# Seven block products in place of eight for every other pair of row tiles in an MLP's second product

## The chip, the cores and the metric

One core of a Trainium2 chip runs the whole program. The metric is the device time of one execution in microseconds (us). The kernel before took 634.06 us (median of 3 runs, 633.57 to 634.90). One more execution was recorded by the profiler; every row below is from it.

## The reference

Two layers of a decoder trunk on one sequence of 256 tokens with 1024 channels, in float32. Each layer adds an attention mixer's output and then an MLP's output to x. The change is in the MLP:

```python
def sqrelu_mlp(hn, w1, w2):
    return jnp.square(jax.nn.relu(hn @ w1)) @ w2
...
x = x + mix
x = x + sqrelu_mlp(rms_norm(x, norm_mlp[i]), mlp_w1[i], mlp_w2[i])
```

`w1` is 1024 x 4096 and `w2` is 4096 x 1024. Layer 0's mixer joins sparse and differential attention, layer 1's is block-sparse attention; both have an input and an output projection.

## The kernel before, in words

**Numbers in two parts.** Every operand of a matmul is split into a high part, which the matmul's format holds exactly, and a low rest. A product a·b is then three matmuls into one PSUM bank: ah·bh, ah·bl and al·bh (`mm3`, L532 to L536). For a weight block of 128x1024 the split is one ScalarE copy to `whi` (L475) and one VectorE subtraction to `wlo` (L478), in `splits`. Pairs of such tiles are slots (`parts`, six of them, and spare halves of `mT` or `xT`, which is why some rows say `mTh`/`mTl` for a weight). `loads` (L452) brings the blocks, 512 KB each, through SP's queue into five `raw` tiles in the order in which `_blocks` lays them out.

**The MLP** (`mlp`, L1357). The 4096 hidden channels are 16 tiles of 256. The first product makes a tile's hidden values transposed, 256 channels by 256 tokens, in one bank: two columns of 128 channels, each 8 steps of `mm3` with 256 columns moving, 48 matmuls (`cols_T`, L614). `square` (L1362) then takes the bank through ReLU (ScalarE), the square's high part (ScalarE, L1370), the whole square (GpSimd, L1371) and the low part (VectorE, L1373). The second product takes a tile's 256 rows of `w2` as two blocks of 128x1024. With two halves of 128 tokens (t) and two halves of 512 output columns (n) that is 2 x 2 x 2 = 8 block products of 128x128 by 128x512, each one `mm3`: 24 matmuls into four banks, one for each (t, n) (`row_mm`, L684). The rows of tile i follow the first product of tile i + 1. The last three tiles (`TAIL`) are kept back and are done (t, n) by (t, n), so that each bank is added to x (`add_to_x`, L1303) and the next stage can begin on it.

**What sets the order.** The program is written once as generators, and a planner (`Plan`) plays it through when the kernel is built: each step has an engine, a cost, what it depends on and an urgency; of the ready steps an engine takes the lowest urgency first. What comes out is a fixed order for each engine. Weight splits have urgency -1 when they are needed soon (`URGENT`) and 3 otherwise. In `out_proj` (L1316), which ends a mixer, the rows of tokens 128 to 255 have the urgency 1 + `LATER[layer]` against 1 for the others (L167, L1341).

**The start.** Until weights are there, TensorE multiplies zeros (`WARM`, L502, and `keep_on`, L907, one at a time at the lowest urgency and an assumed 0.23 us each).

Of the kernel before, what the change touches and what calls it, by code (L numbers as in the profile page):

```python
# [21 lines left out]
F32 = mybir.dt.float32  # L22
# [51 lines left out]
def _blocks(ins):  # L74
# [44 lines left out]

    def mlp(l):  # L120
        up, down = f["mlp_w1"][l], f["mlp_w2"][l]
        last = FF // 256 - TAIL
        out.extend([n(up, 0, 4, span(0, 512)), n(up, 4, 8, span(0, 512)), r(down, 0)])
# [4 lines left out]
        out.extend(r(down, i) for i in range(last, FF // 256))  # L128

# [8 lines left out]
    cut = []  # L138
    for b in out:
# [3 lines left out]
    return cut  # L143


def _lay_out(ins):
    f = {k: np.asarray(ins[k]) for k in ins}
    blocks = _blocks(ins)
# [9 lines left out]
    for i, nm in enumerate(("ev_lam_q1", "ev_lam_q2", "ev_lam_k1", "ev_lam_k2")):  # L158
# [3 lines left out]
            "prm": prm, "gs": gs, "cst": _constants(), "eye": np.eye(128, dtype=np.float32)}, [b.shape[1] for b in blocks]  # L162
# [4 lines left out]
SECOND, ROOM, LATER = 5, (4, 5), (0, 0.05)  # L167
# [148 lines left out]
class Slots:  # L316
# [5 lines left out]
    def get(self, n=1):  # L322
        ev = Event()
        self.waiting.append((ev, n))
# [25 lines left out]
    def serve(self):  # L350
        while self.waiting and len(self.items) >= self.waiting[0][1]:
            ev, n = self.waiting.pop(0)
            got, self.items = self.items[:n], self.items[n:]
# [10 lines left out]
def trunk_kernel(ctx: ExitStack, tc: tile.TileContext, x, w, prm_d, gs, cst_d, eye, out, widths):  # L364
    nc = tc.nc

# [62 lines left out]
    class Piece:  # L429
        count, current, uses = 0, 0, 0  # L430

        def __init__(self):
            self.p, self.ready, self.slots = Piece.count, Event(), parts
            Piece.count += 1

        def use(self):
            Piece.current = max(Piece.current, self.p)
            Piece.uses += 1

# [20 lines left out]

    def splits():
        for p, n in enumerate(widths):
            pc = pieces[p]
            yield loaded[p]
            got = pc.slots.get()
# [416 lines left out]
    KL = acts.tile([128, 2, 2, S], F32R, name="KL")  # L882
    KZ = acts.tile([128, 2, 2, S], F32R, name="KZ")
# [17 lines left out]
    def first_norms():  # L901
        def keep_on():
# [3 lines left out]
            while Piece.uses < KEEP:  # L906
                yield pe(0.23, lambda: nc.tensor.matmul(banks[1].t, z[:, :128], z, start=True, stop=True), u=9)  # L907
# [449 lines left out]
    def mlp(src, x_ready, nxt):  # L1357

        NI = FF // 256
        hs = [Event() for _ in range(NI)]  # L1360

        def square(i, b, deps, slots):  # L1362
            got = pbuf.get(2)
            tgot = tbuf.get()
            yield [got, tgot]
            r, sq = got.value
            hh, hl = tgot.value
# [223 lines left out]
```

## Time and profile before

| | us |
|---|---|
| median of 3 runs | 634.06 |
| the profiled execution | 634.41 |
| its span in the trace | 632.6 |
| TensorE busy | 620.1 |
| VectorE busy | 404.5 |
| ScalarE busy | 361.7 |
| GpSimd busy | 80.4 |

The profiled execution's own time is 1.8 us over its span, which is the time around the first and last instruction. A row of the timeline gives an instruction's start and duration; the duration reaches past the moment at which the engine takes the next instruction, so starts that follow each other are closer than durations say. Line numbers are those of the listing above.

### The profile page before, as it was taken

How to read it: one execution, taken by the hardware profiler on the slowest of the kernel's cores; microseconds unless marked ns; L12 is line 12 of the kernel's file. 1: busy time of each engine (PE TensorE's matmuls, PEld its weight loads, DVE VectorE, ACT ScalarE, POOL GpSimd, SP SyncE). 2: the span in 40 equal slices, each digit the busy share in tenths (PEclk: the TensorE clock that was granted, in tenths of full speed). 3: DMA queues.
4: the chain of work that ended last, by engine and by line, in shares of the span. 5: the costliest groups of instructions: out<-in, count | busy, mean ns of one | idle time of the engine just before them, and what ended most of it. 6: DMA issues, size and time to landing. Idle time of an engine off the chain costs nothing.

```text
span 632.6 us, 10575 instructions
## 1 busy us (share of the span) xinstructions
PE 620.1 (98%) x4046; PEld 562.6 (89%) x4046; DVE 404.5 (64%) x722; ACT 361.7 (57%) x649; POOL 80.4 (13%) x109
## 2 busy tenths in 40 slices
PE   9999999999999999999999999999999999999995
PEld 7999989887899898998988999988889899898994
DVE  5898899868554544545467588885964454554434
ACT  5779587656644545444444488773864544445421
POOL 2031031210200101011120012010020101001111
PEclk9999999999999999999999999999999999999998
DMA  8864633426665576565626443350786556565501
GB/s 324 283 244 133 202 101 110 176 92 204 222 204 196 168 204 192 191 186 205 189 82 212 168 137 131 130 189 17 229 271 214 185 189 188 181 209 167 166 1 67
DMA packets 32274, 110.03 MB, mean 174 GB/s; under 512 B 3408, under 2 KB 5728, under 8 KB 32224
## 3 DMA queue, kind: packets, MB, share of 16 engines
q1 hardware_dynamic: 31360, 106.74, 51.7%
q0 software_dynamic: 576, 2.10, 1.0%
q8 instruction: 31, 0.51, 0.3%
q10 hardware_dynamic: 288, 0.52, 0.2%
q14 instruction: 19, 0.16, 0.1%
HBM read 108.28 MB, written 1.07 MB: 173 GB/s over the span
## 4 chain that ended last, share of the span: by engine, by line
PE 86%; DVE 7%; ACT 4%; issue 2%; POOL 1%; POOLq 0%; DVEq 0%; ACTq 0%
PE ps L535 27%; PE ps L536 27%; PE ps L534 26%; DVE wlo L478 2%; PE ps L763 2%; PE ps L797 1%; ACT P L777 1%; PE ps L597 1%; PE ps L907 1%; PE ps L502 1%; ACT whi L475 1%; DVE P L773 1%; DVE G L974 0%; DVE Tl L525 0%; DVE x L1308 0%
## 5 line engine op out<-in xcount | busy, mean ns | idle before, releaser
L478 DVE TENSOR_TENSOR wlo<-raw,whi 128x1024 fp32r<-128x1024 f32 (+1 forms) x157 | 190.3, 1220 | 71.8 <-ACT whi L475 71.3
L475 ACT ACTIVATE whi<-raw 128x1024 fp32r<-128x1024 f32 (+1 forms) x157 | 163.3, 1051 | 93.2 <-PE ps L536 62.3
L534 PE MATMUL ps<-xTh,whi 128*128 128x256 f32 x592 | 169.1, 286 | 0.0
L536 PE MATMUL ps<-xTh,wlo 128*128 128x256 f32 x592 | 166.3, 281 | 0.0
L535 PE MATMUL ps<-xTl,whi 128*128 128x256 f32 x592 | 166.2, 281 | 0.0
L535 PEld LDWEIGHTS ps<-xTl,whi 128*128 128x128 f32 x592 | 111.7, 189 | 0.6
L534 PEld LDWEIGHTS ps<-xTh,whi 128*128 128x128 f32 x592 | 111.6, 188 | 0.6
L536 PEld LDWEIGHTS ps<-xTh,wlo 128*128 128x128 f32 x592 | 111.5, 188 | 0.0
L1371 POOL TENSOR_TENSOR P<-P 128x512 f32<-128x512 f32 x32 | 35.8, 1119 | 321.5 <-ACT P L1368 321.5
L478 DVE TENSOR_TENSOR mTl<-raw,mTh 128x1024 fp32r<-128x1024 f32 x34 | 42.5, 1249 | 22.9 <-ACT mTh L475 22.9
L475 ACT ACTIVATE mTh<-raw 128x1024 fp32r<-128x1024 f32 x34 | 36.1, 1062 | 29.7 <-PE ps L535 20.3
L1368 ACT ACTIVATE P<-ps 128x512 f32<-128x512 f32 x32 | 19.1, 598 | 52.3 <-PE ps L536 52.3
L1373 DVE TENSOR_TENSOR Tl<-P,Th 128x512 fp32r<-128x512 f32 x22 | 15.2, 692 | 50.2 <-POOL P L1371 50.2
L536 PE MATMUL ps<-whi,Tl 128*128 128x512 f32 x120 | 46.9, 390 | 0.0
L535 PE MATMUL ps<-wlo,Th 128*128 128x512 f32 x120 | 46.9, 390 | 0.0
L534 PE MATMUL ps<-whi,Th 128*128 128x512 f32 x120 | 46.8, 390 | 0.0
L777 ACT ACTIVATE P<-P,nm 128x128 f32<-128x128 f32 x80 | 35.4, 446 | 14.1 <-DVE nm L773 13.9
L535 PE MATMUL ps<-xTl,mTh 128*128 128x256 f32 (+1 forms) x128 | 37.9, 296 | 1.1 <-DVE xTl L478 1.1
L534 PE MATMUL ps<-xTh,mTh 128*128 128x256 f32 (+1 forms) x128 | 38.1, 297 | 0.0
L536 PE MATMUL ps<-xTh,mTl 128*128 128x256 f32 (+1 forms) x128 | 37.8, 295 | 0.0
L534 PE MATMUL ps<-whi,xTh 128*128 128x512 f32 (+1 forms) x88 | 34.3, 390 | 0.0
L535 PE MATMUL ps<-wlo,xTh 128*128 128x512 f32 (+1 forms) x88 | 33.1, 376 | 0.0
(221 smaller groups left out, 1196.7 us busy)
## 6 DMA issues: line engine op xcount, KB each, us to landing
raw<-in_w_dram SPq DMA_DIRECT2D x192, 512.0 KB, 4.1
gB<-in_gs_dram POOLq DMA_DIRECT2D x4, 512.0 KB, 4.0
x<-in_x_dram SPq DMA_DIRECT2D x2, 512.0 KB, 5.2
B<-ud SPq DMA_DIRECT2D x1, 1024.0 KB, 7.6
B<-ud SPq DMA_DIRECT2D x2, 512.0 KB, 9.1
raw<-in_w_dram SPq DMA_DIRECT2D x2, 420.0 KB, 7.0
gB<-in_gs_dram SPq DMA_DIRECT2D x1, 512.0 KB, 5.3
out_dram<-P SPq DMA_DIRECT2D x2, 256.0 KB, 2.1
```

Source lines behind the costliest of these rows:

```text
L475: nc.scalar.activation(pc.hi[:, :n], raw[:, :n], AF.Copy)
L478: nc.vector.tensor_tensor(pc.lo[:, :n], raw[:, :n], pc.hi[:, :n].bitcast(F32), OP.subtract)
L502: pe(0.43, lambda: nc.tensor.matmul(banks[7].t, tbuf.items[1][0][:, :128], tbuf.items[1][0], start=True, stop=True), zero_e)
L534: nc.tensor.matmul(out_, ah, bh, start=start, stop=False)
L535: nc.tensor.matmul(out_, ah, bl, start=False, stop=False)
L536: nc.tensor.matmul(out_, al, bh, start=False, stop=stop)
L597: nc.tensor.transpose(p[:, 128 * k:128 * k + 128], xs[:, 128 * k:128 * k + 128], ident)
L763: nc.tensor.matmul(ps[:, 128 * qt:128 * qt + nk], q[:, par, ts], k[i][:, par, :nk], start=i == 0, stop=i == 1)
L777: nc.scalar.activation(P[:, c], P[:, c], AF.Exp, bias=nm[:, qt:qt + 1], scale=-1.0, accum_out=sums[:, qt:qt + 1])
L1368: e = act(t_act(512), lambda: nc.scalar.activation(r, b.t, AF.Relu), got, *deps)
L1371: g = pool(1.225, lambda: nc.gpsimd.tensor_tensor(sq, r, r, OP.mult), e)
L1373: h = dve(t_dve(512), lambda: nc.vector.tensor_tensor(hl, sq, hh.bitcast(F32), OP.subtract), f, g)
```

## The change

For the tiles with odd number below 13 (1, 3, 5, 7, 9, 11 of each MLP; "fused" in the code) the 2 x 2 x 2 block product is done with seven block products in place of eight. With a(t,k) the hidden blocks and b(k,n) the weight blocks, VectorE forms t1 = b01 - b00, t3 = b11 - b01, t2 = b11 - t1 and t4 = b10 - t2 in place in the raw tiles, and s1 = a10 + a11, s2 = s1 - a00, s3 = a00 - a10 and s4 = a01 - s2. The products a00·b00, a01·b10, s1·t1, s3·t3, s2·t2, s4·b11 and a11·t4 go to seven banks; an output block is the sum of some of them.

For the even tiles below 13 ("apart") the eight products remain. They go to four of the seven banks (those of b10, t4, t1 and b11); since t1's bank is added to both halves of the tokens, the product for b11's bank takes a(0,k) - a(1,k), which VectorE forms.

The rest that changes with it:

- `square` has no GpSimd step: VectorE multiplies r by r. It writes into two slots in `G0` and `G1` (`hbuf`), and splits the sums too.
- The seven banks leave one for the first product, which runs one tile further ahead; the weight blocks are laid out in that order. One more weight slot lies in `KL` and `G1` (`spare_w`).
- When a fused or apart product is over, b00's, t1's, t2's and t3's banks are added to x by 4, 2, 3 and 2 operations of 128x512 on VectorE, ahead of the last three tiles; those go into b10's, b11's and t4's banks and one fresh bank.
- A zero product at the start is planned at 0.43 us before 6.3 us.
- `LATER` for layer 1 is -0.05 in place of 0.05.

```diff
-            if i <= last:
-                out.append(r(down, i - 1))
+            if i - 2 < last:
+                out.append(r(down, i - 2))
+                if _fused(i - 2):
+                    fused.add(len(out) - 1)
...
+def _fused(i):
+    return i % 2 == 1 and i < FF // 256 - TAIL
...
-SECOND, ROOM, LATER = 5, (4, 5), (0, 0.05)
+SECOND, ROOM, LATER = 5, (4, 5), (0, -0.05)
...
+    def split_pair(p):
...
+        def place(k, names, src, deps):
+            hi, lo = k
+            n = 512 * len(names)
+            e = act(t_act(n, False), lambda: nc.scalar.activation(hi[:, :n], src, AF.Copy), *deps, u=u)
+            f = dve(t_dve(n), lambda: nc.vector.tensor_tensor(lo[:, :n], src, hi[:, :n].bitcast(F32), OP.subtract), e, u=u)
...
+        def total(dst, a, b, *deps):
+            return dve(t_dve(512), lambda: nc.vector.tensor_tensor(dst, a, b, OP.subtract), *deps, u=u)
...
+        f1 = place(k.value, ["b00"], r1[:, :512], [k, loaded[p]])
+        e1 = total(r1[:, :512], r1[:, 512:], r1[:, :512], f1)
...
+        f2 = place(k.value, ["b10", "b11"], r2, [k, loaded[p + 1]])
+        e3 = total(r1[:, 512:], r2[:, 512:], r1[:, 512:], e1, loaded[p + 1])
+        e2 = total(r2[:, 512:], r2[:, 512:], r1[:, :512], e3, f2)
+        e4 = total(r2[:, :512], r2[:, :512], r2[:, 512:], e2)
...
+        raws.put(r1, [place(k.value, ["t1", "t3"], r1, [k, e1, e3]), e2])
...
+        raws.put(r2, [place(k.value, ["t4", "t2"], r2, [k, e4])])
...
-                yield pe(0.23, lambda: nc.tensor.matmul(banks[1].t, z[:, :128], z, start=True, stop=True), u=9)
+                yield pe(0.43 if plan.now < 6.3 else 0.23, lambda: nc.tensor.matmul(banks[1].t, z[:, :128], z, start=True, stop=True), u=9)
...
-            f = act(t_act(512, False), lambda: nc.scalar.activation(hh, r, AF.Square), e, tgot)
-            g = pool(1.225, lambda: nc.gpsimd.tensor_tensor(sq, r, r, OP.mult), e)
...
-            h = dve(t_dve(512), lambda: nc.vector.tensor_tensor(hl, sq, hh.bitcast(F32), OP.subtract), f, g)
...
+            f = act(t_act(512, False), lambda: nc.scalar.activation(hh[:, :512], r, AF.Square), e, hgot)
+            e = dve(t_dve(512), lambda: v(sq, r, r, OP.mult), e, got)
+            pbuf.put(r, [f, e])
+            h = dve(t_dve(512), lambda: v(hl[:, :512], sq, hh[:, :512].bitcast(F32), OP.subtract), f, e)
...
+            if _fused(i):
+                n = 512
+                a00, a10, a01, a11 = (sq[:, 128 * j:128 * j + 128] for j in range(4))
+                s1, s2, s3, s4 = (ss[:, 128 * j:128 * j + 128] for j in range(4))
+                for dst, x_, y_, op in ((s1, a10, a11, OP.add), (s2, s1, a00, OP.subtract), (s3, a00, a10, OP.subtract),
+                                        (s4, a01, s2, OP.subtract)):
+                    e = dve(t_dve(128), lambda dst=dst, x_=x_, y_=y_, op=op: v(dst, x_, y_, op), e)
+            else:
+                n = 256
+                d = sq.rearrange("p (k t c) -> p k t c", k=2, t=2)
+                e = dve(t_dve(256), lambda: v(ss[:, :256].rearrange("p (k c) -> p k c", k=2), d[:, :, 0], d[:, :, 1], OP.subtract), e)
+            f2 = act(t_act(n, False), lambda: nc.scalar.activation(hh[:, 512:512 + n], ss[:, :n], AF.Copy), e, hgot)
+            h2 = dve(t_dve(n), lambda: v(hl[:, 512:512 + n], ss[:, :n], hh[:, 512:512 + n].bitcast(F32), OP.subtract), f2)
...
+        TERMS = (("b00", 0, (0, 1, 2, 3)), ("b10", 2, (0,)), ("t1", 4, (1, 3)), ("t3", 6, (2, 3)),
+                 ("t2", 5, (1, 2, 3)), ("b11", 7, (1,)), ("t4", 3, (2,)))
...
+        def apart(i, pcs):
...
+                       for nm, col, n in (("b10", 2 * a, 0), ("t4", 2 * a + 1, 0), ("t1", 2 * a + 1, 1), ("b11", 4 + a, 1))]
...
+        def fused(i, pc):
+            ends = []
+            for nm, col, _ in TERMS:
...
+                product(nm, i, col, op, pc.block(nm), i == LAST[nm])
...
+        for i in range(NI - 2):
+            if i + 2 < NI:
                 got = bank_a.get()
                 yield got
                 evs = [got] + [cols_T(src, got.value, next_piece(), col) for col in range(2)]
-                plan.spawn(square(i + 1, got.value, evs, bank_a))
+                plan.spawn(square(i + 2, got.value, evs, bank_a))
...
+            if i < NI - TAIL:
+                two = [next_piece(), next_piece()]
+                if _fused(i):
+                    fused(i, two[0])
+                else:
+                    apart(i, two)
...
+                def add(b=b, t=t, n=n):
+                    c = slice(512 * n, 512 * n + 512)
+                    nc.vector.scalar_tensor_tensor(X[t][:, c], b.t, rs2[t][0], X[t][:, c], op0=OP.mult, op1=OP.add)
```

TensorE issues 40 matmuls fewer (36 of 128x512 in the two MLPs and four zero products at the start), VectorE 214 operations more, ScalarE 50 more, GpSimd 32 fewer; SP's order of transfers is the same. Up to the first MLP the orders of ScalarE, VectorE and GpSimd are unchanged.

**The start, on TensorE.** L502 and L907 are the zero products of the kernel before, L589 and L998 those of the change; L597 and L684 are the transposes of the normed tokens, L534 and L621 the first matmul on weights. Before:

```order
L502 MATMUL ps7_117<-Th1_87 128x512 x10
L907 MATMUL ps1_111<-Th1_87 128x512 x10
L597 MATMUL ps4_114<-ident_121,P0_99 128x128 x4
L907 MATMUL ps1_111<-Th1_87 128x512
L597 MATMUL ps5_115<-ident_121,P1_100 128x128 x4
L907 MATMUL ps1_111<-Th1_87 128x512 x8
L534 MATMUL ps0_110<-whi0_74,xTh_104 128x280
```

and with the change:

```order
L589 MATMUL ps7_117<-Th1_87 128x512 x10
L998 MATMUL ps1_111<-Th1_87 128x512 x6
L684 MATMUL ps4_114<-ident_121,P0_99 128x128 x4
L998 MATMUL ps1_111<-Th1_87 128x512
L684 MATMUL ps5_115<-ident_121,P1_100 128x128 x4
L998 MATMUL ps1_111<-Th1_87 128x512 x7
L621 MATMUL ps0_110<-whi0_74,xTh_104 128x280
```

Six zero products stand ahead of the first transposes where ten stood, and seven in place of eight ahead of the first matmul on weights.

**Inside the first MLP, on VectorE.** Before, one tile's work between two others, L478 being the low part of a weight block and L1373 that of the hidden tile:

```order
L478 TENSOR_TENSOR mTl_91<-raw3_97,mTh_90 128x1024
L478 TENSOR_TENSOR wlo1_81<-raw4_98,whi1_75 128x1024
L478 TENSOR_TENSOR mTl_91<-raw0_94,mTh_90 128x1024
L1373 TENSOR_TENSOR Tl1_89<-P1_100,Th1_87 128x512
L478 TENSOR_TENSOR wlo2_82<-raw1_95,whi2_76 128x1024
```

and with the change the larger part of one fused tile. L1479 is the square, L1494 the four sums of hidden blocks, L1481 and L1501 the low parts of the squares and of the sums, L513 the low part of a pair of weight blocks, L522 the differences of weight blocks:

```order
L1479 TENSOR_TENSOR P4_103<-P2_101 128x512
L1494 TENSOR_TENSOR P0_99<-P4_103 128x128
L1494 TENSOR_TENSOR P0_99<-P0_99,P4_103 128x128
L1481 TENSOR_TENSOR G1_93<-P4_103,G1_93 128x512
L1494 TENSOR_TENSOR P0_99<-P4_103 128x128
L1494 TENSOR_TENSOR P0_99<-P4_103,P0_99 128x128
L513 TENSOR_TENSOR wlo5_85<-raw2_96,whi5_79 128x1024
L1501 TENSOR_TENSOR G1_93<-P0_99,G1_93 128x512
L522 TENSOR_TENSOR raw1_95<-raw2_96,raw1_95 128x512
L522 TENSOR_TENSOR raw2_96<-raw2_96,raw1_95 128x512
L522 TENSOR_TENSOR raw2_96<-raw2_96 128x512
L513 TENSOR_TENSOR wlo1_81<-raw1_95,whi1_75 128x1024
```

Ahead of these stand the low part of b00 and the first difference, and behind them the low part of t4 and t2: 15 operations for one fused tile, beside the two weight splits of the first product, where three stood.

**The end of layer 1's output projection, on TensorE.** `mTh`/`mTl` are the attention's outputs, `xTh`/`xTl` the normed tokens for the MLP, L597 and L684 the transposes that make them, and ps1 and ps0 the banks of the MLP's first product. Before, the last transposes of tokens follow twelve matmuls of that product, the last of which stand here:

```order
L534 MATMUL ps1_111<-whi2_76,xTh_104 128x512
L535 MATMUL ps1_111<-wlo2_82,xTh_104 128x512
L536 MATMUL ps1_111<-whi2_76,xTl_105 128x512
L597 MATMUL ps5_115<-ident_121,P0_99 128x128 x4
L534 MATMUL ps0_110<-whi1_75,xTh_104 128x512
```

and with the change, from the output projection's last product on:

```order
L621 MATMUL ps1_111<-whi2_76,mTh_90 128x512
L622 MATMUL ps1_111<-wlo2_82,mTh_90 128x512
L623 MATMUL ps1_111<-whi2_76,mTl_91 128x512
L621 MATMUL ps0_110<-KL_130,xTh_104 128x512
L622 MATMUL ps0_110<-G1_93,xTh_104 128x512
L623 MATMUL ps0_110<-KL_130,xTl_105 128x512
L621 MATMUL ps0_110<-KL_130,xTh_104 128x512
L622 MATMUL ps0_110<-G1_93,xTh_104 128x512
L623 MATMUL ps0_110<-KL_130,xTl_105 128x512
L684 MATMUL ps7_117<-ident_121,P2_101 128x128 x4
```

Six matmuls stand between the last output product and the last transposes where twelve stood.

## Rows read from the trace of the kernel before

**Rows 1.** Page, section 1: busy us (share of the span) and instructions per engine

```profile
PE 620.1 (98%) x4046; PEld 562.6 (89%) x4046; DVE 404.5 (64%) x722; ACT 361.7 (57%) x649; POOL 80.4 (13%) x109
```

**Rows 2.** Waits of TensorE: waiter, releaser, us in total, times, longest

```profile
PE ps L597 <- DVE P L581: 1.2, 1, 1.2
```

**Rows 3.** Windows, both MLPs: PE, PEld, DVE, ACT, POOL busy; clock; DMA share; GB/s

```profile
168.00:312.00 144.00, 144.00 (x937) 131.66 (x936) 71.44 (x65) 70.29 (x79) 14.48 (x14) 1.00 0.60 192
467.00:614.00 147.00, 147.00 (x950) 134.11 (x949) 70.79 (x66) 68.91 (x78) 15.55 (x15) 1.00 0.54 172
```

**Rows 4.** Timeline of TensorE in the first MLP: start, us, engine, line, instruction

```profile
239.84 0.39 PE L534 MATMUL ps<-whi,G 128*128 128x512 f32 x1
...
243.93 0.28 PE L534 MATMUL ps<-xTh,whi 128*128 128x256 f32 x1
...
249.61 0.40 PE L534 MATMUL ps<-mTh,Th 128*128 128x512 f32 x1
```

**Rows 5.** Lines by form, whole run: instruction, count, busy us, mean ns, idle before

```profile
L478 DVE TENSOR_TENSOR wlo<-raw,whi 128x1024 fp32r<-128x1024 f32 x154 | 187.6, 1226 | 70.8 <-ACT whi L475 70.3
...
L475 ACT ACTIVATE whi<-raw 128x1024 fp32r<-128x1024 f32 x154 | 160.9, 1055 | 90.0 <-PE ps L536 62.3 <-PE ps L535 23.5 <-issue 2.1
...
L1373 DVE TENSOR_TENSOR Tl<-P,Th 128x512 fp32r<-128x512 f32 x22 | 15.2, 692 | 50.2 <-POOL P L1371 50.2
...
L1310 DVE SCALAR_TENSOR_TENSOR x<-ps,rs,x 128x512 f32<-128x512 f32 x8 | 6.0, 749 | 11.7 <-PE ps L536 11.7
...
L525 DVE TENSOR_TENSOR mTl<-ps,mTh 128x256 fp32r<-128x256 f32 x12 | 5.0, 422 | 4.8 <-ACT mTh L519 4.5
```

**Rows 6.** Timeline of VectorE, an early 128-column operation

```profile
19.45 0.23 DVE L735 TENSOR_TENSOR lp<-prm 128x128 f32<-128x128 f32 x1
```

**Rows 7.** Timeline of VectorE, start of the second MLP's first product

```profile
448.07 2.35 DVE L478 TENSOR_TENSOR wlo<-raw,whi 128x1024 fp32r<-128x1024 f32 x2
450.33 0.68 DVE L525 TENSOR_TENSOR xTl<-ps,xTh 128x512 fp32r<-128x512 f32 x1
450.93 1.21 DVE L478 TENSOR_TENSOR wlo<-raw,whi 128x1024 fp32r<-128x1024 f32 x1
```

**Rows 8.** Tile raw, first MLP: idle before its instructions (us, times) by releaser

```profile
  PE ps L536: 29.9, 26
  ACT whi L475: 29.2, 24
```

**Rows 9.** Timeline of the first 12 us, TensorE and VectorE

```profile
5.87 3.24 PE L907 MATMUL ps<-Th 128*128 128x512 f32 x10
...
6.60 1.42 DVE L923 SCALAR_TENSOR_TENSOR P<-x,rs,gB 128x512 f32<-128x512 f32 x2 [1.71 <-DMA gB<-in_gs_dram]
...
8.95 0.60 PE L597 MATMUL ps<-ident,P 128*128 128x128 f32 x4
...
10.22 0.69 DVE L525 TENSOR_TENSOR xTl<-ps,xTh 128x512 fp32r<-128x512 f32 x1
...
11.91 0.29 PE L534 MATMUL ps<-whi,xTh 128*128 128x280 f32 x1
```

**Rows 10.** Timeline, second MLP, up to the first product's first matmul

```profile
456.16 2.46 DVE L478 TENSOR_TENSOR wlo<-raw,whi 128x1024 fp32r<-128x1024 f32 x2 [0.34 <-ACT whi L475]
459.46 1.23 DVE L478 TENSOR_TENSOR wlo<-raw,whi 128x1024 fp32r<-128x1024 f32 x1 [0.84 <-ACT whi L475]
461.62 0.69 DVE L1373 TENSOR_TENSOR Tl<-P,Th 128x512 fp32r<-128x512 f32 x1 [0.93 <-POOL P L1371]
...
462.68 0.40 PE L534 MATMUL ps<-whi,Th 128*128 128x512 f32 x1
```

**Rows 11.** Windows, the same place in the first MLP

```profile
155.30:163.90 8.60, 8.60 (x58) 7.78 (x57) 4.96 (x6) 6.50 (x8) 1.59 (x1) 1.00 0.90 274
```

**Rows 12.** Timeline around the output projection's end in layer 0

```profile
146.02 0.69 DVE L581 TENSOR_TENSOR P<-x,gB 128x512 f32<-128x512 f32 x1
...
146.86 0.63 PE L597 MATMUL ps<-ident,P 128*128 128x128 f32 x4 [1.16 <-DVE P L581]
```

More of the change, by code (lines that the diff above doesn't have):

```diff
@@ L137, in _blocks @@
     mlp(1)
-    cut = []
-    for b in out:
+    cut, kinds = [], []
+    for i, b in enumerate(out):
         b = np.ascontiguousarray(b).reshape(128, -1)
@@ L350, in serve @@
     def serve(self):
-        while self.waiting and len(self.items) >= self.waiting[0][1]:
-            ev, n = self.waiting.pop(0)
-            got, self.items = self.items[:n], self.items[n:]
+        while self.waiting:
+            ev, n, only = self.waiting[0]
+            got = [i for i in self.items if only is None or only(i)][:n]
+            if len(got) < n:
+                return
+            self.waiting.pop(0)
+            self.items = [i for i in self.items if not any(i is g for g in got)]
             self.plan.fire(ev, "slot", got if n > 1 else got[0])
@@ L438, in use, with block, got, done @@
             Piece.uses += 1
+        def block(self, name):
+            return self.blocks.setdefault(name, Event())
+        def got(self, names, f):
+            for nm in names:
+                ev = self.block(nm)
+                plan.when([f], None, lambda ev=ev: plan.fire(ev, DVE))
+        def done(self, name, ev):
+            k, names = self.left[name]
+            names.remove(name)
+            self.ends.setdefault(id(k), []).append(ev)
+            if not names:
+                parts.put(k, self.ends[id(k)])
         def release(self, ev):
@@ L463, in splits @@
             pc = pieces[p]
+            if kinds[p] == "pair":
+                yield from split_pair(p)
+            if kinds[p] in ("pair", "second"):
+                continue
             yield loaded[p]
-            got = pc.slots.get()
+            got = pc.slots.get(only=None if kinds[p] or pc.slots is not parts else usual)
             yield got
@@ L1390, in turned @@
                 first.append(g)
-                yield g
+                plan.fire(asked)
+            yield first[0]
             bs = first[0].value
@@ L1423, in give, with product, emit @@
-        def give(i):
-            evs = prev[0] + prev[1]
-            plan.when([hs[i]], None, lambda: tbuf.put(hs[i].value, evs))
-        for i in range(NI):
-            if i >= 1 and i + 1 < NI:
+        def give(i, evs, slots):
+            plan.when([hs[i]], None, lambda: slots.put(hs[i].value, evs))
+        def product(nm, i, col, op, ready, last):
+            def emit():
+                c = slice(128 * col, 128 * col + 128)
+                mm3(acc[nm][0].t, tuple(a[:, c] for a in ha[i].value), op(), not begun[nm], last)
+                begun[nm] = True
+            prev[nm] = pe(0.695, emit, prev[nm], ready, (ha if col < 4 else hs)[i], u=1)
+            return prev[nm]
@@ new lines, in apart, with op @@
+        def apart(i, pcs):
+            ends = []
+            for a, pc in enumerate(pcs):
+                def op(n, pc=pc):
+                    pc.use()
+                    return pc.hi[:, 512 * n:512 * n + 512], pc.lo[:, 512 * n:512 * n + 512]
+                own = [product(nm, i, col, lambda n=n, op=op: op(n), pc.ready,
+                               nm == "t1" and i == LAST[nm] and a == 1)
+                       for nm, col, n in (("b10", 2 * a, 0), ("t4", 2 * a + 1, 0), ("t1", 2 * a + 1, 1), ("b11", 4 + a, 1))]
+                pc.release(plan.all(own))
+                ends += own
+            give(i, ends, hbuf)
@@ L1539, in program @@
         yield from out_proj(o_e, plan.all(reads), f3)
-        yield from mlp(box3["src"], box3["ready"], final)
+        yield from mlp(box3["src"], box3["ready"], final, flat(o_e))
     fin = {}
```

158 lines of the change are left out of this document (117 added, 41 removed).

## The prediction

> **What bounds the kernel now.** I read the page first: TensorE is busy for 620.1 us, 98% of the span, VectorE for 404.5 [rows 1]. A busy TensorE need not be the bound, so I asked next what it waits for: the longest wait of all, behind the zero products at the start, is 1.2 us, once [rows 2]. Then the windows of the stretches that the change rewrites. In 168 to 312 us TensorE is busy for all of 144.00 us, at a granted clock of 1.00 (2.4 GHz), and VectorE for 71.44, ScalarE for 70.29; the second MLP reads the same [rows 3]. So in both MLPs TensorE's work is the time, and a matmul that goes is gained as long as VectorE, which gets the new work, still delivers in time. That is the whole question. About 1.8 us of the 634.41 us lie outside the span and stay.
>
> **TensorE: 36 matmuls go.** The price of one is its distance to the next, not its duration. In the timeline 18 matmuls of 512 columns start between 239.84 and 243.93 us, 0.227 us each, though each is recorded with 0.39; and 48 of 256 columns between 243.93 and 249.61, 0.118 each [rows 4]. Twelve fused tiles save 3 of 512 columns each: 36 x 0.227 = **8.2 us**. For two tiles (one apart, one fused) TensorE then needs 96 x 0.118 + 45 x 0.227 = 21.6 us, against 22.3 now.
>
> **VectorE: does it keep up?** For two tiles it now has 8 weight splits of 1.226 us and 2 low parts of 0.692 [rows 5]: 11.2 us, which is what the window shows (71.44 / 144 x 22.3 = 11.1). With the change it has 9 operations of 1024 columns, 10 of 512 (one split, four differences, two squares, three low parts), 2 of 256 and 4 of 128. If each holds the engine for its recorded duration, with 0.422 for 256 columns [rows 5] and 0.23 for 128 [rows 6], that is 9 x 1.226 + 10 x 0.692 + 2 x 0.422 + 4 x 0.23 = 19.7 us. If it holds it for the distance of starts, 1.13 for 1024 columns (two between 448.07 and 450.33) and 0.60 for 512 (450.33 to 450.93) [rows 7], it is 18.0 us. Either is below 21.6, so VectorE goes from half to 83 to 91% of the stretch and leaves 1.9 to 3.6 us per two tiles. I take 18.0 as the nearer, because independent operations are most of the list, and cost the steady part at nothing; what covers it is TensorE's 21.6 us, and beyond that each further microsecond would count in full.
>
> A rule speaks against this. The Trainium skill (VectorE: DVE Perf Modes, section "The DRAIN you can't avoid") says that the next operation does not start until the pipe of the one before is empty. By it the load is the sum of the durations, 19.7 us, and half of the margin is gone; the rows differ from it, since the split that follows at 450.93 starts 0.08 us before the recorded end of the one ahead of it. The sum of this forecast is the same by both, the first rival below is not.
>
> ScalarE has 4 operations more for two tiles (a split's half and whole, two copies of sums); at 1.055 each at most [rows 5] its 10.9 us become 15.1 of 21.6. GpSimd loses its squares. The transfers are the same bytes in the same order, and the DMA share of 0.60 in the MLP leaves room [rows 3].
>
> **Order on VectorE.** It takes its work in the written order, so a low part that waits for ScalarE's high part holds everything behind it. In the first MLP VectorE stands idle for 29.2 us in 24 waits for `whi`, 1.2 each, and ScalarE itself 29.9 us for TensorE, which frees the weight slots [rows 8]. Now these waits cost nothing, as TensorE waits for none of this work. With 1.9 to 3.6 us to spare they may come to cost; the planner's extra slot and its order are meant for that, so I take nothing, and the first two rivals price it.
>
> **The start.** The ten zero products ahead of the first transposes run from 5.87 to 8.95 us, 0.31 each, while the transposes' operand, the first of two 0.7 us operations begun at 6.60, is there by 7.4 [rows 9]. So they delay it, and with four fewer the transposes come 1.2 us earlier. The first matmul on weights starts at 11.91; its low part of the tokens is there at 10.22 + 0.69 = 10.9 [rows 9], so 1.0 is open at once. What of it is left after the first mixer, where TensorE waits for VectorE now and then, lies between 0 and 1.3 (4 x 0.31); I take **0.8 us**, near the upper end, since the longest wait that could take it up is the 1.2 us of [rows 2], and that comes behind the whole mixer.
>
> **The beginning of the second product.** VectorE has six more operations of 512 columns and one of 256 ahead of tile 0's low part: 6 x 0.60 + 0.42 = 4.0 us. In the second MLP that low part now starts at 461.62 and ends at 462.31, and its matmul starts at 462.68 [rows 10]. The change puts nine matmuls of 256 columns (1.1 us) ahead of it, so it must be there at 463.74. VectorE's idle time just before, 0.34 + 0.84 + 0.93 = 2.1 us [rows 10], takes up half of the 4.0: ready at 464.2, 0.5 us late. If none of it can be filled it is 2.6 late. At the same place of the first MLP VectorE is busy for 5 of 8.6 us [rows 11]; the idle rest nearly holds the 4.0, and with the 1.1 us I take nothing there. The ends are 0 to 2.6 us for each MLP.
>
> **The end of layer 1's output projection.** The six matmuls left between the last output product and the last transposes are 1.4 us. In layer 0, where the order has always been like this, the operand for the transposes is formed at 146.02 and TensorE stood still for 1.16 us [rows 12]. From the end of the output matmuls the way is an addition (0.75 by its nearest row [rows 5]), this operation (0.69) and the handover (146.71 to 146.86), 1.6 us, so 0.2 us show; at most 1.2. A late start there gives VectorE the same time, so I put both places together at **0.5 us**, with 0 and 6.4 as ends.
>
> **The end of an MLP.** 11 additions of 0.749 us [rows 5] are 8.2 us of VectorE. They lie beside the last first product and the last three tiles, 48 x 0.118 + 72 x 0.227 = 22.0 us of TensorE, with at most six weight splits (7.4) and six operations for hidden tiles (4.2): 19.8. Hidden; without that cover the next stage would be late by what exceeds it. The end of the program, after the last matmul, is not touched.
>
> **The sum.** 634.41 - 8.2 - 0.8 + 0.5 = 625.9 for the profiled execution. The median is 0.35 lower, so I predict **625.6 us**.
>
> **The rivals.**
> - *VectorE is late at single places.* Every operation holds the engine for its duration, waits for ScalarE come on top, and TensorE stands still before some fused tiles. For: 19.7 of 21.6 us, and waits of 1.2 us that exist now. Against: the waits today are those of an engine with nothing to do. It decides where more than 1.9 us of waits fall into two tiles; at 0.4 us for each fused tile it is 12 x 0.4 = 4.8, so 630.4. This is also what the page's rule would make of it. Chance 16%.
> - *VectorE becomes the bound* (slower than before). Its low parts wait for high parts whose slots TensorE frees only when the previous product is over, so that the engines take turns. Place: every pair of tiles below 13. Price: with three waits of 1.2 us two tiles take 19.7 + 3.6 = 23.3 us against 22.3 now; 1.0 more x 12 = 12 us, and the start's gain stays: 645. It decides from 2.6 us of waits in two tiles on, more than two of today's. Chance 5%.
> - *The gain is given back whole*, as the first rival with 0.65 us for each fused tile: within 0.2% of before, that is 632.8 to 635.3. The 0.2% is about what a measurement of this kernel can tell from no change. Chance 4%.
> - That the change doesn't do what it says is excluded for the matmuls: 36 are gone from the order.
>
> **How the numbers follow.** The forecast has 75%: 624.0 (the start's whole 1.3 and no loss, and some 0.5 for the second mixer's new order) to 627.5. The first rival reaches from there to 632.8. For 8 times in 10 I take 624.0 to 630.5, which leaves out the upper part of the first rival and the two others. Faster: 75 + 16 = 91%; same 4%; slower 5%.
>
> **What would show it.** Right: TensorE busy near 611 us with the spacing of 0.227 kept, no wait before a fused product in the list of waits, VectorE near 530 us in all (404.5 + 126 of new work) and at 83 to 91% in the MLPs, GpSimd near 45, the first transposes near 7.7 us. Wrong: waits of TensorE for the low parts of weights or sums in the MLPs of more than 2 us together, or a busy VectorE without gaps in them; a first matmul on weights at 11.9; or a gap before the last transposes at the end of layer 1's mixer.

## The result and the profile after

The changed kernel takes **626.39 us** (median of 4 runs, 626.21 to 626.54) against 634.14 for the one before in the same comparison: a ratio of 0.9878, 95% interval 0.9866 to 0.9890. That is 7.7 us less; 8.5 were forecast, and the time lies in the range. The profiled execution took 626.42 us with a span of 624.6.

The page's busy times per engine, after, answer to [rows 1]:

```profile
PE 610.8 (98%) x4006; PEld 553.9 (89%) x4006; DVE 513.8 (82%) x936; ACT 387.5 (62%) x699; POOL 47.1 (8%) x77
```

TensorE has 9.3 us less work, VectorE 109 more, and GpSimd stands at 47 (45 were forecast). For VectorE 126 were forecast, the sum of durations. This view counts an overlap once, and 214 new operations with some 0.08 us of overlap each, as in [rows 7], give an estimate of 17 us, the difference. TensorE's share is 98% as before. Whether VectorE's new work is waited for stands in TensorE's waits (waiter, releaser, us in total, times, longest):

```profile
PE ps L684 <- DMA ident<-in_eye_dram: 1.4, 1, 1.4
PE ps L589 <- DVE Th L587: 1.4, 1, 1.4
PE ps L684 <- DVE P L668: 1.2, 1, 1.2
PE ps L622 <- DVE xTl L565: 1.1, 2, 0.7
```

None of these is in the two MLPs' windows below. The third is the wait of [rows 2] at the same place in layer 0; only the first, at the start, is new. Then the windows of the two MLPs (columns as in [rows 3]) and what VectorE waits for in the first of them:

```profile
165.00:295.00 130.00, 130.00 (x849) 118.85 (x848) 111.75 (x150) 77.53 (x96) 0.00 (x0) 1.00 0.61 199
461.00:591.00 130.00, 130.00 (x848) 118.93 (x847) 110.65 (x147) 77.61 (x98) 0.00 (x0) 1.00 0.60 197
```
```profile
DVE wlo L565 <- ACT whi L562: 12.4, 10, 2.2
DVE G L565 <- ACT KL L562: 2.9, 2, 2.2
```

TensorE is busy all the time, as before. VectorE went from half to 86%, 18.6 of the 21.65 us of two tiles. It still stands idle for 3.0 us of them, 2.5 in waits for ScalarE's high parts (12.4 and, for the slot in `KL`, 2.9 in six pairs of tiles), and TensorE does not wait for it. The gain sits where it was forecast: from the last transposes at the beginning of the first MLP to the first ones behind it the kernel before needs 162.46 us (160.96 to 323.42 in its timeline), the changed one 158.67:

```profile
160.38 0.60 PE L1528 MATMUL ps<-ident,P 128*128 128x128 f32 x4
...
319.05 1.03 PE L684 MATMUL ps<-ident,P 128*128 128x128 f32 x8
```

Of the span's 8.0 us the two MLPs give 7.7; the rest is the start's 0.6 less 0.2 to 0.3 at layer 1's output projection. Both of these are taken up below.

### The profile page after: what moved, and what is told of

Its sections match the earlier page's. It is cut to its first block, busy times and chain, and to the rows that moved or that the text cites. A ratio compares the mean times of both kernels' runs of the same rounds, so it can differ in the third digit from the quotient of the medians.

```text
span 624.6 us, 10690 instructions
## 1 busy us (share of the span) xinstructions
PE 610.8 (98%) x4006; PEld 553.9 (89%) x4006; DVE 513.8 (82%) x936; ACT 387.5 (62%) x699; POOL 47.1 (8%) x77
## 4 chain that ended last, share of the span: by engine, by line
PE 86%; DVE 6%; ACT 4%; issue 2%; DMA 1%; POOL 0%; SPq 0%; POOLq 0%; DVEq 0%; ACTq 0%
PE ps L622 27%; PE ps L623 27%; PE ps L621 26%; DVE wlo L565 2%; PE ps L850 2%; PE ps L884 2%; ACT P L864 1%; PE ps L684 1%; DMA ident<-in_eye_dram 1%; ACT whi L562 1%; PE ps L998 1%; DVE x L1399 1%; DVE G L1065 0%; DVE P L921 0%; DVE P L860 0%
## 5 line engine op out<-in xcount | busy, mean ns | idle before, releaser
L621 PE MATMUL ps<-xTh,whi 128*128 128x256 f32 x520 | 149.0, 287 | 0.0
L623 PE MATMUL ps<-xTh,wlo 128*128 128x256 f32 x520 | 146.1, 281 | 0.0
L622 PE MATMUL ps<-xTl,whi 128*128 128x256 f32 x520 | 146.0, 281 | 0.0
L622 PEld LDWEIGHTS ps<-xTl,whi 128*128 128x128 f32 x520 | 98.1, 189 | 0.8
L621 PEld LDWEIGHTS ps<-xTh,whi 128*128 128x128 f32 x520 | 98.0, 188 | 0.8
L623 PEld LDWEIGHTS ps<-xTh,wlo 128*128 128x128 f32 x520 | 98.0, 188 | 0.0
L623 PE MATMUL ps<-whi,G 128*128 128x512 f32 x141 | 55.2, 391 | 0.0
L622 PE MATMUL ps<-wlo,G 128*128 128x512 f32 x141 | 55.1, 391 | 0.0
L621 PE MATMUL ps<-whi,G 128*128 128x512 f32 x141 | 55.1, 390 | 0.0
L512 ACT ACTIVATE whi<-raw 128x1024 fp32r<-128x1024 f32 (+1 forms) x32 | 30.9, 964 | 23.5 <-PE ps L623 14.5
L621 PE MATMUL ps<-xTh,mTh 128*128 128x256 f32 (+1 forms) x144 | 42.4, 294 | 0.0
L1468 ACT ACTIVATE P<-ps 128x512 f32<-128x512 f32 x32 | 18.7, 592 | 37.9 <-PE ps L623 37.9
L513 DVE TENSOR_TENSOR wlo<-raw,whi 128x1024 fp32r<-128x1024 f32 (+1 forms) x32 | 35.3, 1103 | 0.8 <-ACT whi L512 0.6
L621 PE MATMUL ps<-whi,xTh 128*128 128x512 f32 (+1 forms) x84 | 32.9, 391 | 0.0
L623 PEld LDWEIGHTS ps<-whi,G 128*128 128x128 f32 x141 | 26.4, 188 | 5.9 <-DVE G L1481 0.2
L623 PE MATMUL ps<-whi,xTl 128*128 128x512 f32 (+1 forms) x84 | 31.5, 375 | 0.0
```

What stands on the lines that cost most here:

```text
L512: e = act(t_act(n, False), lambda: nc.scalar.activation(hi[:, :n], src, AF.Copy), *deps, u=u)
L513: f = dve(t_dve(n), lambda: nc.vector.tensor_tensor(lo[:, :n], src, hi[:, :n].bitcast(F32), OP.subtract), e, u=u)
L621: nc.tensor.matmul(out_, ah, bh, start=start, stop=False)
L622: nc.tensor.matmul(out_, ah, bl, start=False, stop=False)
L623: nc.tensor.matmul(out_, al, bh, start=False, stop=stop)
```

## The experiments

Each was compared with the kernel before in runs beside it; that kernel took 633.9 us there, and 634.4 beside experiment 4. So a difference between two experiments carries some tenths of a microsecond. The diffs are against the changed kernel.

**1. No fused tile.**

```diff
-    return i % 2 == 1 and i < FF // 256 - TAIL
+    return False
```
(With it, three banks that then hold nothing are not added to x.)

> The changed kernel with no fused tile: all 13 tiles below the last three are multiplied apart (8 products), everything else of the change stays (first product two tiles ahead, squares on VectorE, differences of 256 columns, fewer zero products at the start). Theory (TensorE's work is the time in both MLPs, the new work of VectorE costs nothing): 36 matmuls of 512 columns come back at 0.227 to 0.229 us, +8.2, so 634.0 to 634.7 us, with no wait of TensorE inside the MLPs. Rival (the fused tiles lost time to VectorE, 0.4 us each): the matmuls come back but these losses go, +8.2 - 4.8, so near 629.8. Second rival (a part of the gain came from the other edits): clearly under 633.6.

Measured: 635.52 us, a ratio of 1.0025 (1.0016 to 1.0034): 9.1 more than with the change, 0.8 above the theory's range. No wait of TensorE in the MLPs. The rivals are out: the fused tiles lose nothing to VectorE, and no other edit brings a part of the gain. Experiment 4 shows where the 0.8 comes from.

**2. The zero products of the start as before.**

```diff
-                yield pe(0.43 if plan.now < 6.3 else 0.23, lambda: ...
+                yield pe(0.23, lambda: ...
```

> The changed kernel with the zero products of the start planned at 0.23 us all along, as before: ten instead of six ahead of the first transposes, eight instead of seven behind the second. Theory (what is gained at the start is kept to the end): first transposes back at 8.9 to 9.0 us, first matmul on weights at 11.9 instead of 11.13, and the time 0.55 us longer (between 0.5 and 0.8), 626.9 to 627.2. Rival (later waits of the first mixer take up the start's gain): 626.4, no change. The forecast's own price, if its 0.8 had been right: 627.2.

Measured: 626.37 us, the same as the change, each in four runs. So fewer zero products bring nothing in these runs, and my theory's number is wrong. The timeline of this kernel shows why:

```profile
5.87 2.59 PE L998 MATMUL ps<-Th 128*128 128x512 f32 x10
8.30 0.60 PE L684 MATMUL ps<-ident,P 128*128 128x128 f32 x4
```

The same ten zero products that in [rows 9] took from 5.87 to 8.95, 0.31 each in the mean, take 0.24 here. A zero product takes 0.43 us at first and 0.23 later, and the moment of that fall is another in each execution: 4.7 us in the changed kernel's profile, 6.1 here, 7.6 in the one of before. In each trace this is also the moment at which the record of the granted clock begins, with 1.00. Ahead of it there is no record, but 0.43 us is what a matmul of 512 columns takes where the granted clock is 0.50, or 1.2 GHz (455.23 to 455.65 us in experiment 3). The late transposes of [rows 9] were an accident of that one execution. And with six zero products the next wait stands behind them, here in the changed kernel:

```profile
5.37 1.55 PE L998 MATMUL ps<-Th 128*128 128x512 f32 x6
8.37 0.63 PE L684 MATMUL ps<-ident,P 128*128 128x128 f32 x4 [1.45 <-DMA ident<-in_eye_dram]
```

The trace of the kernel before has this transfer too. Issued at 2.10 us, it landed 6.2 us later (the last number of the second row), at 8.3, so that at most 0.7 us could be had there:

```profile
2.10 0.43 SPq L409 DMA_DIRECT2D ident<-in_eye_dram  x1
```
```profile
ident<-in_eye_dram SPq DMA_DIRECT2D x1, 64.0 KB, 6.2
```

One part of the theory holds: what differs at the start is kept. In all three profiles the last transposes at the beginning of the first MLP follow the first ones of the start by 152.0 us (8.95 and 160.96 before, 8.37 and 160.38 with the change, 8.30 and 160.28 here).

**3. Layer 1's output projection in the old order.**

```diff
-SECOND, ROOM, LATER = 5, (4, 5), (0, -0.05)
+SECOND, ROOM, LATER = 5, (4, 5), (0, 0.05)
```

> The changed kernel with layer 1's output projection ordered as before (LATER back to 0.05). Theory: the last transposes of that projection no longer come 0.2 to 0.3 us after the matmuls ahead of them (TensorE stands still there at 442.5 us in the changed kernel), nothing else moves: 0.2 to 0.3 us faster, 626.1 to 626.2. Rival (the old order makes the transposes wait less but brings the first low part of the second product too late): TensorE waits for it at the beginning of the second product, up to 2.6 us slower, 626.6 to 629.0. Third case: no difference over 0.1 us.

Measured: 632.01 us (0.9975 of before, 0.9966 to 0.9984), 5.6 slower than the change. Theory and rival were both too small, and neither had the place: both expected the last transposes of the tokens (L684) to wait less, and these wait longest. TensorE's waits in this kernel's timeline between 450 and 462 us:

```profile
451.33 0.65 PE L684 MATMUL ps<-ident,P 128*128 128x128 f32 x4 [1.70 <-DVE P L668]
453.10 0.50 PE L621 MATMUL ps<-whi,xTh 128*128 128x512 f32 x1 [1.11 <-ACT xTh L606]
454.20 0.80 PE L623 MATMUL ps<-whi,xTl 128*128 128x512 f32 x1 [0.36 <-DVE ms L655]
461.22 0.66 PE L1528 MATMUL ps<-ident,P 128*128 128x128 f32 x4 [1.49 <-ACT P L1513]
```

These are 4.7 us, and TensorE's clock falls besides (same columns as above):

```profile
450.00:452.00 2.00, 0.65 (x4) 0.42 (x4) 1.97 (x3) 2.00 (x3) 0.42 (x1) 1.00 0.83 236
452.00:454.00 2.00, 0.74 (x2) 0.30 (x2) 2.00 (x3) 2.00 (x4) 0.15 (x1) 1.00 0.76 260
454.00:456.00 2.00, 1.80 (x4) 1.49 (x5) 1.97 (x5) 0.63 (x1) 0.00 (x0) 0.53 0.82 236
456.00:458.00 2.00, 2.00 (x7) 1.55 (x6) 1.96 (x3) 0.00 (x0) 0.00 (x0) 0.61 0.96 344
458.00:460.00 2.00, 1.72 (x14) 1.47 (x12) 0.39 (x1) 0.38 (x1) 0.00 (x0) 1.00 0.91 354
```

After 2.6 idle us in 450 to 454 (busy 0.65 and 0.74) the granted clock falls to 0.50, 1.2 GHz, for 3.4 us, from 454.1 to 457.5. VectorE is busy for 3.3 of the 8 us before 448 and for 7.4 of the 8 after, so its work comes in one lump. Before 448 it waits for the high part that ScalarE writes into `KL`, and ScalarE's ReLU of the first product, which stands ahead of that in ScalarE's order, waits for TensorE:

```profile
445.17 0.60 ACT L1513 ACTIVATE P<-ps 128x512 f32<-128x512 f32 x1 [3.90 <-PE ps L623]
```
```profile
446.94 1.23 DVE L565 TENSOR_TENSOR G<-raw,KL 128x1024 fp32r<-128x1024 f32 x1 [4.41 <-ACT KL L562]
```

Whether this chain is the whole cause was not tried apart. In the changed kernel there is a gap of 0.29 at this place (442.80 less 442.28 and the usual 0.23):

```profile
442.28 0.39 PE L623 MATMUL ps<-KL,xTl 128*128 128x512 f32 x1
442.80 0.66 PE L684 MATMUL ps<-ident,P 128*128 128x128 f32 x4
```

**4. No fused tile, and the old order there** (edits 1 and 3 together).

> The kernel without fused tiles (first experiment) with layer 1's output projection ordered as before (LATER back to 0.05): both old habits of the place where the third experiment lost 5.6 us. Theory (there it is the work that the fused tiles put in front of VectorE, sums of blocks and more low parts, that made the second product start late): without fused tiles the old order costs nothing, as in the kernel before; 633.9 to 635.5 us, no gap of TensorE over 1.2 us between 440 and 470 us. Rival (the first product running two tiles ahead, or the transfers of weights in the new order, need the early transposes): 4 to 6 us slower than the first experiment, 639 to 641.

Measured: 634.61 us against 634.36 for before (1.0005, 0.9996 to 1.0015), and no gap of TensorE at this place. The theory holds: the old order costs much only with fused tiles. The new order alone costs 0.9 us in a kernel without them (experiment 1; 1.3 if each is taken against the kernel before beside it), which is the excess there. Against this kernel the change gains 8.2 us (8.0 in the same way): 36 matmuls at 0.22 to 0.23.

**5. Three more squares for each fused tile on VectorE.**

```diff
             e = dve(t_dve(512), lambda: v(sq, r, r, OP.mult), e, got)
+            for _ in range(3 if _fused(i) else 0):
+                e = dve(t_dve(512), lambda: v(sq, r, r, OP.mult), e)
```

> The changed kernel with the square of every fused tile multiplied three times more on VectorE (3 operations of 512 columns that write the same values again, 0.60 us from start to start, 0.69 recorded): 1.8 to 2.1 us more for two tiles. In the changed kernel VectorE is busy for 111.3 of 130.0 us in the first MLP, so it stands idle for 3.1 us of each 21.65 us (two tiles), 2.1 of it in waits for the high part of weights. Theory (all of the idle time is room, waits included): 626.4, at most 0.5 more. Rival (the waits for ScalarE are no room, 1.0 us is left): 0.8 to 1.1 us too much for two tiles, 12 times, 636 to 640 us.

Measured: 626.21 us, no change. VectorE's window in the first MLP, and its waits:

```profile
165.00:295.00 130.00, 130.00 (x849) 118.84 (x848) 122.62 (x167) 77.06 (x96) 0.00 (x0) 1.00 0.58 197
```
```profile
DVE wlo L565 <- ACT whi L562: 3.5, 5, 1.1
```

At 94% TensorE still is busy throughout, and VectorE's waits for `whi` shrink from 12.4 to 3.5 us: they were part of the room, not a load of their own.

**6. Six more.** (The same edit with 6.)

> The same with six more squares for every fused tile, 3.6 to 4.1 us more for two tiles. Theory (the room is the 3.1 us): 0.5 to 1.0 us too much for two tiles, 12 times, 632.5 to 638.5 us, TensorE waiting for low parts in both MLPs, VectorE without gaps in them. Rival (the waits are no room): 2.6 to 3.1 us too much, 657 to 664 us. If it stays at 626.4 to 627.5, the planner's order has found room that the windows do not show.

Measured: 652.38 us, between theory and rival, so a miss by 14 us. The room ends between the 1.8 us of experiment 5 and the 4.1 of this one, which fits the theory's 3.1; what lies beyond costs much more than it said. Starts of apart tiles, two tiles apart, in this kernel:

```profile
231.24 0.39 PE L621 MATMUL ps<-whi,G 128*128 128x512 f32 x1
...
254.13 0.39 PE L621 MATMUL ps<-whi,G 128*128 128x512 f32 x1
...
277.67 0.39 PE L621 MATMUL ps<-whi,G 128*128 128x512 f32 x1
...
300.81 0.39 PE L621 MATMUL ps<-KL,G 128*128 128x512 f32 x1
```

From 231.24 on two tiles take 23.2 us in the mean, 1.5 more than in the changed kernel, and VectorE is busy for 22.35 of them; up to here that is 5.4 us (300.81 against 295.42). But the first MLP is over 12.5 us later (the transposes behind it at 331.53 instead of 319.05). The other 7 fall behind the last apart tile, where VectorE, late by now, still has its sums for the last fused tile, the additions and the last low parts to do:

```profile
320.42 0.79 PE L623 MATMUL ps<-whi,G 128*128 128x512 f32 x1 [3.17 <-DVE G L1483]
```
```profile
316.00:318.00 2.00, 0.49 (x1) 0.19 (x1) 2.00 (x3) 0.00 (x0) 0.00 (x0) 1.00 0.17 33
318.00:320.00 2.00, 0.00 (x0) 0.00 (x0) 1.90 (x3) 0.00 (x0) 0.00 (x0) 0.77 0.97 301
320.00:322.00 2.00, 1.58 (x4) 1.29 (x5) 2.00 (x3) 0.00 (x0) 0.00 (x0) 0.50 0.86 281
...
324.00:326.00 2.00, 2.00 (x6) 1.61 (x5) 0.00 (x0) 0.05 (x1) 0.24 (x1) 0.52 0.81 250
```

TensorE stands still from 317 to 320, and the granted clock is 0.50 (1.2 GHz) from 319.1 to 325.9.

**7. Two of three tiles fused** (nine in each MLP).

```diff
-    return i % 2 == 1 and i < FF // 256 - TAIL
+    return i % 3 != 2 and i < FF // 256 - TAIL
```

> The changed kernel with two of three tiles fused (tiles 0, 1, 3, 4, 6, 7, 9, 10, 12: nine instead of six in each MLP). 18 further matmuls of 512 columns go: at 0.2287 us 4.1 us less, if VectorE keeps up. Its work for an apart tile is 6.8 us (78.9 of 130 us in the kernel without fused tiles, 11.16 us a tile), for a fused one 18.55 - 6.8 = 11.8, so 30.3 us for three tiles against TensorE's 2 x 10.48 + 11.16 = 32.1: 94%. Theory (VectorE costs nothing below 100%): 622.3 us. Rival (its waits for ScalarE's high parts, 2.1 us for two tiles, are no room): 33.4 against 32.1, 1.3 us lost for three tiles, 8.7 times, 11 in all, near 633.

Measured: **622.29 us**, ratio 0.9818 (0.9803 to 0.9832): the theory's number, and the fastest kernel of this study, 4.1 us below the change (3.9 below experiment 5, which ran beside it).

```profile
165.00:295.00 130.00, 130.00 (x850) 118.99 (x849) 123.93 (x172) 81.61 (x104) 0.00 (x0) 1.00 0.59 197
461.00:591.00 130.00, 130.00 (x848) 118.95 (x847) 125.09 (x172) 83.97 (x105) 0.00 (x0) 1.00 0.58 199
```

VectorE is at 95 to 96% and TensorE still waits for nothing.

**8. Three of four** (ten; `i % 4 != 3`).

> The changed kernel with three of four tiles fused (0, 1, 2, 4, 5, 6, 8, 9, 10, 12: ten in each MLP), squares on VectorE. 24 matmuls of 512 columns less than the change: 5.5 us. VectorE needs 3 x 11.8 + 6.8 = 42.2 us for four tiles, TensorE 3 x 10.48 + 11.16 = 42.6: 99%. Theory (no cost below 100%, but nothing left for single waits and for the additions at the end of an MLP, which a VectorE that is behind cannot hide): between 620.9 and 625. Rival (it keeps up all the same): 620.9. Second rival (as with six more squares, a VectorE that is behind pays at the end of each MLP, some 6 us each): 630 or more.

Measured: 626.08 us, 3.8 slower than nine tiles with six matmuls less, 1 us over the theory's range. Four tiles take 43.4 us (a matmul of the same kind starts at 239.46 and 282.85), not TensorE's 42.6:

```profile
239.46:282.85 43.39, 42.87 (x282) 38.97 (x280) 41.45 (x59) 26.63 (x34) 0.00 (x0) 1.00 0.60 196
```
```profile
PE ps L621 <- ACT P L1468: 2.8, 4, 1.1
```
```profile
ACT whi L512 <- DVE raw L522: 14.1, 10, 2.7
```

VectorE is busy for 41.45 of them, which is 97% of TensorE's 42.6 and less than the 42.2 that I took, and it stands idle for 1.9. So the cost sets in before VectorE's busy time reaches TensorE's. TensorE's longest new wait is for ScalarE's ReLU out of the first product's banks (L1468), 2.8 us in both MLPs together, and ScalarE is itself held up by VectorE: in 165 to 295 us it waits 33 us for results of VectorE, most of all for the differences of weight blocks (L522), and 14.5 for transfers of weights. How much the transfers add was not tried.

**9. All 13.** (`i < FF // 256 - TAIL`)

> The changed kernel with all 13 tiles below the last three fused. 42 further matmuls go, 9.6 us of TensorE; VectorE needs 11.8 us for a tile, TensorE 10.48. Theory (VectorE becomes the bound from 100% on and then counts in full): 13 tiles take 153.1 us instead of 6 x 21.65 + 11.16 = 141.1, twice 12.0 more, near 650 us, VectorE busy without gaps in the MLPs and TensorE waiting for weights. Rival (VectorE's operations overlap more closely when it never waits, 0.60 and 1.13 us from start to start: 11.2 us a tile): 145.6 instead of 141.1, near 635.5. Third case (TensorE still is the bound): 616.8.

Measured: 652.59 us, the theory's 650 and not the rivals'. Five tiles from 207.34 to 265.04 take 11.5 us each, against TensorE's 10.48, and VectorE is busy for 98% of the window. So VectorE is the bound:

```profile
165.00:295.00 130.00, 121.50 (x772) 107.96 (x771) 127.84 (x188) 80.17 (x102) 0.00 (x0) 0.99 0.50 168
```

The number meets the theory in part by luck. A tile takes 0.3 us less than the theory's 11.8, and TensorE's granted clock falls to 0.50 three times (at 284.3, 335.5 and 571.0, for 3.4, 6.8 and 3.4 us), which the theory did not have.

**10. The squares back on GpSimd.**

```diff
-            e = dve(t_dve(512), lambda: v(sq, r, r, OP.mult), e, got)
+            e = pool(1.225, lambda: nc.gpsimd.tensor_tensor(sq, r, r, OP.mult), e, got)
```

> The changed kernel with the squares of the hidden tiles back on GpSimd, as before the change, nothing else. VectorE has two operations of 512 columns less for two tiles (1.2 to 1.4 of 18.55 us), GpSimd two of 1.07 us more. Theory (VectorE's load costs nothing below TensorE's 21.65 us for two tiles): no difference, 626.2 to 626.6 us. Rival (moving the squares is a part of the gain, or GpSimd's squares slow VectorE's operations down): 627 or more, VectorE's operations of 1024 columns longer than the 1.22 us of the changed kernel.

Measured: 626.51 us, the same; yet the second half of the rival shows in the durations, below.

**11. Eleven tiles fused** (`i % 6 != 5`) **and the squares on GpSimd.**

> Eleven tiles fused in each MLP (all below 13 but 5 and 11) and the squares on GpSimd. 30 matmuls of 512 columns less than the change: 6.9 us. VectorE needs 0.65 us less for each tile: 5 x 11.1 + 6.1 = 61.6 us for six tiles, TensorE 5 x 10.48 + 11.16 = 63.6: 97%. Theory (the bound changes engines at 100% of VectorE, wherever the work is taken off): 619.5 to 620.5 us. Rival (runs of five fused tiles use up the room faster than one apart tile gives it back, or GpSimd and VectorE slow each other down): TensorE waits in the MLPs, 623 to 632.

Measured: 637.03 us (1.0052, 1.0040 to 1.0065), worse than the rival. VectorE is at 99% of the window and TensorE waits, most of all for ScalarE's ReLU out of the first product's banks (L1468), as in experiment 8:

```profile
165.00:295.00 130.00, 124.20 (x796) 111.22 (x795) 128.43 (x175) 80.72 (x102) 21.21 (x12) 1.00 0.54 181
```
```profile
PE ps L621 <- ACT P L1468: 11.0, 11, 1.5
```

**12. The identity's transfer one place earlier, fewer zero products behind the transposes.**

```diff
-    ident_e = load(ident, eye, u=0.4)
+    ident_e = load(ident, eye, u=0.1)
```
(With it, every zero product is planned at 0.43.)

> The changed kernel with the transfer of the transposes' identity issued ahead of the first weights (one place earlier on SyncE) and zero products planned at 0.43 us all along (six instead of seven behind the transposes). Theory (the identity's transfer is what the first transposes wait for at 8.37 us): it lands 0.4 to 0.6 us earlier, first transposes at 7.8 to 8.0, first matmul on weights at 10.6 to 10.8 instead of 11.13, time 0.3 to 0.5 us shorter, 625.9 to 626.1. Rival (the transposes wait for something else, or the first low part of the tokens waits on VectorE behind the first weights' split): transposes earlier or not, the first matmul on weights stays at 11.1 and the time at 626.4.

Measured: 626.43 us, no change. The first transposes do come at 7.09, so that transfer was what they waited for, and the first matmul on weights at 10.30, but the matmuls then wait for the tokens' high part (0.74 us) and low part (0.21), and the third of them starts at 11.39, as in the changed kernel. The rival holds in its second form: behind the wait removed stands another.

## Why the prediction was right, and where it was not

- **TensorE, -8.2.** Right. The matmuls' price of 0.22 to 0.23 us is shown twice: 8.0 to 8.2 us for 36 (change against experiment 4), 3.9 to 4.1 for 18 (experiment 7).
- **VectorE keeps up at no cost.** Right, and shown by experiment 5, which adds 1.8 to 2.1 us for two tiles and changes nothing. The load was sized rightly too: for two tiles VectorE is busy for 18.6 us, between the 18.0 by the distances of starts and the 19.7 by durations and nearer the first. For a fused tile alone, with its two splits for the first product, the two counts are 11.4 (5 x 1.13 + 8 x 0.60 + 4 x 0.23) and 12.6 (with 1.226 and 0.692); where VectorE is the bound it takes 11.5 (experiment 9). The Trainium skill's rule (VectorE: DVE Perf Modes, "The DRAIN you can't avoid") gave the 19.7. The prediction used half of it: the Trainium skill adds in the same section that a next operation that is not held starts earlier. Experiment 9 agrees with that half. The first rival, which was to follow from the rule, did not come. What failed is "beyond that each further microsecond would count in full": experiment 8 pays already at 97% of TensorE's time, and in experiment 6 VectorE's busy time for two tiles exceeds TensorE's by 0.7 us (22.35 against 21.65), which in full would be 8 us for twelve pairs, and 26 were paid.
- **Waits in order, 0.** Right. The 2.5 us that VectorE waits for ScalarE in two tiles are above the 1.9 from which the first rival was to decide; they cost nothing, because they shrink when there is more to do (those for `whi` from 12.4 to 3.5 us in experiment 5). Its point of decision was wrong: idle time that an engine spends waiting ahead of its need is room.
- **The start, -0.8.** Wrong: it is 0 (experiment 2). The step that failed is "so they delay it, and with four fewer the transposes come 1.2 us earlier". The pace of the ten zero products in [rows 9] belonged to that execution alone. And behind them stood the identity's transfer, which the prediction left out although the trace of before has it: it landed at 8.3 us, 0.7 and not 1.2 ahead of the transposes. That all of a late start is kept was right, but the 0.6 us by which the two profiles differ there are no gain of the edit.
- **Beginning of the second product and layer 1's junction, +0.5.** The sum nearly held: 0.29 us, and no wait at either MLP's beginning. But the forecast read the new order mainly as a cost of 0.2. It is what makes the fused tiles fit: without it 5.6 us are lost there (experiment 3). The range's end of 6.4 allowed for such a size, but by another mechanism.
- **The end of an MLP, hidden.** Right for the change. Experiment 6 shows what is due when VectorE comes late to it: 7 of the 12.5 us lost in the first MLP.
- **The rivals.** The bound does change to VectorE, but not at the change's 86%: experiments 8, 6 and 9, where TensorE waits, have VectorE's busy time at 97, 103 and 108% of TensorE's time for the same tiles.

So 8.2 us of matmuls went, and 7.7 arrived in the two MLPs of the profiled executions. The half microsecond between them lies in the 715 matmuls of 512 columns that are left there (18 fewer in each MLP): they start 0.2290 us apart in the mean, where before it was 0.2283. Why they are further apart stays open. The medians differ by 7.7 as well; the junction's 0.29 and what the start of each execution gave or took are in them.

## What to carry to other kernels

Work may be moved from a saturated engine to a half idle one at full gain, as long as the second engine's busy time stays a few per cent below the first one's time for the same stretch: 94 to 96% was free here (experiments 5 and 7), 97% cost 5 us (experiment 8, against its 620.9) and 103% cost 26 (experiment 6). Count operations that do not depend on each other by the distance of their starts, take waits that shrink under load as room, and see that the stretch ends with the second engine not behind, since its backlog is paid there, with the clock on top. An edit of order that looks like a small cost may be what carries the large one, so undo it alone before calling it harmless; and a start that is read from one execution should be read from a second.

## What the runs showed of the hardware

GpSimd and VectorE slow each other down when both multiply or subtract two tensors. In experiment 10 (start, us, engine, instruction):

```profile
188.50 2.06 POOL L1479 TENSOR_TENSOR P<-P 128x512 f32<-128x512 f32 x1 [9.99 <-ACT P L1468]
199.14 1.04 POOL L1479 TENSOR_TENSOR P<-P 128x512 f32<-128x512 f32 x1 [8.59 <-ACT P L1468]
```
```profile
189.57 3.20 DVE L565 TENSOR_TENSOR mTl<-raw,mTh 128x1024 fp32r<-128x1024 f32 x2
...
200.04 2.36 DVE L565 TENSOR_TENSOR wlo<-raw,whi 128x1024 fp32r<-128x1024 f32 x2 [2.28 <-ACT whi L562]
```

The square takes 2.06 us beside two splits, which need 3.20 instead of 2.36, and 1.04 while VectorE is idle for nearly all of it. The Trainium skill (GPSIMD Engine Reference, "1. Specifications") says that the two engines share their way to SBUF where a VectorE instruction has two inputs there; the rows agree. With eleven fused tiles a square takes 1.90 us in the mean (12 in the first MLP):

```profile
L1479 POOL TENSOR_TENSOR P<-P 128x512 f32<-128x512 f32 x12 | 22.8, 1899 | 109.4 <-ACT P L1468 105.4 <-ACT G L1478 4.0
```

So taking the squares off VectorE gave back less than their 0.65 us a tile (in experiment 10 its busy time in the first MLP's window falls by 3.1 us, from 111.75 to 108.70, about 0.25 a tile), and did not make the room that experiment 11 counted on; leaving them there, as the change does, costs nothing (experiment 10).

The second thing is the clock: two to three idle microseconds of TensorE were followed by 3.4 us (experiment 3) and 6.8 us (experiment 6) at a granted clock of 0.50, 1.2 GHz, so that a wait there cost more than its own length.
